# Down-projection of a hybrid decoder layer by Strassen's seven products over 1024 tokens

## Chip, cores and metric

One core of a Trainium2 chip runs the whole layer in one launch. The metric is device time in microseconds (us), the median of three runs. TensorE (PE in the profile) does the matrix products, its weight loads stand apart as PEld; VectorE is DVE, ScalarE ACT, GpSimd POOL, and SyncE (SP) issues all DMAs.

## The reference, cut to what matters

2048 tokens of width 1024; all tensors are 32-bit floats. After a mixing part (projection, short convolution, dilated attention, output projection) come the feed-forward and a gated embedding:

```python
h = rmsnorm(x, g_ffn[i])
gate = causal_dwconv3(h @ w_gate[i], ffn_conv_w[i], ffn_conv_b[i])       # 1024 -> 2816
x = x + (jax.nn.silu(gate) * (h @ w_up[i])) @ w_down[i]                  # 2816 -> 1024
ple_gate = jax.nn.sigmoid(rmsnorm(x, g_ple[i]) @ w_ple_gate[i])
x = x + ple_gate * (p[i] @ w_ple_proj[i])
```

## The kernel before

**Products.** Every operand of a product is split in two: `hi`, its rounded copy made by ScalarE (L89), and `lo`, the rest, made by a subtraction (L90) on VectorE or GpSimd. One product of 128x128 by 128x512 then takes three matmuls (`mm3`, L92): hi*hi, hi*lo, lo*hi.

**Stages.** `rest` (L649) runs the stages of the list in L651 to L653. The tokens lie in four chunks of 512 (c = 0 to 3); a half h is two chunks. `gate_up(h)` makes gates and ups of a half by Strassen-Winograd: `left` (L690) makes seven operands of a block of weights (four of them through sums on VectorE, L702), `right` (L715) makes the seven operands of h from four blocks, and `products` (L735) does the seven products of 12 matmuls each. One turn of f (11 turns) is one call of `products` for the gates and one for the ups: 14 products, 168 matmuls. On the way VectorE filters the gates (`taps`, L243: a short copy L247, two steps L255 and L256), adds products to PSUM results (L746, L940, L951) and multiplies up by gate (L949, L952). The result goes to DRAM (`gd`, L953).

**Down.** `down(c)` (L958) takes one chunk. For each half of the 1024 output columns it goes over 22 blocks f of the contraction: the block of `gd` is loaded and split (hi ScalarE, lo VectorE, tiles `g`), a block of `w_down` comes from `stream` (L610; loaded by SP, hi ScalarE, lo GpSimd, tiles `w`), and `tokens_major` (L795) does 4 x 3 = 12 matmuls into four PSUM banks. So four chunks take 4 x 2 x 22 x 12 = 2112 matmuls. At the end of a half VectorE adds the residual from PSUM (L972), SP stores it (L973) and ScalarE sums the squares (L771).

**Background.** `prepare(1)` makes the right operands for the second half (load, `normalize` L781, transposes on TensorE L792, `right`), `prepare_ple` those of `w_ple_gate`. They are generators; `step()` (L808) runs each up to its next yield, four times per half in `down`. `prepare_ple` has four yields, so all of it is issued in the first half of `down(2)`; its seven lo subtractions per block of k are all on GpSimd.

**Order.** The program order is turned into a fixed order for each engine when the kernel is built, by a planner with costs of its own; at run time each engine and the DMA queue take their instructions strictly in this order. Buffers limit how far anyone is ahead: `stream` keeps 3 operands ready, pools hold 5 `w`, 4 `g`, 10 `t`, 4 `s` and 4 `u` tiles, PSUM has 6 banks for products and 2 for transposes.

Of the kernel before, what the change touches and what calls it, by code (L numbers as in the profile page):

```python
# [39 lines left out]
class Layer:  # L40


    def __init__(self, tc, a, out, ctx):
# [14 lines left out]
        self.gd = [d.tile([NF, P, QT], F32, name=f"gd{c}") for c in range(NQ)]  # L58
# [531 lines left out]
    def weight_units(self, stages):  # L590
# [4 lines left out]
        for name, *arg in stages:  # L595
# [9 lines left out]
            elif name == "down":  # L605
                for half in range(2):
                    for u in range(NF // 2):
                        yield pair(a["w_down"], half)[u]

    def stream(self, raws, operand, left, ahead, stages):  # L610
# [3 lines left out]
        def load(src):  # L614
            if src.shape[1] == 2:
                raw = [raws.tile([P, 2, 512], F32, name="raw", tag="raw")]
# [7 lines left out]
        def made():  # L624
            units = self.weight_units(stages)
            following = load(next(units))
            while following:
                raw, src = following, next(units, None)
                following = None if src is None else load(src)
                if len(raw) == 1:  # L630
                    for i in range(2):
# [17 lines left out]
    def rest(self):  # L649
        nc, tc, a = self.nc, self.tc, self.a  # L650
        stages = [("project", (0, 1), (0,)), ("project", (0, 1), (1,)), ("prepare", 0), ("project", (2, 3), (0, 1)),  # L651
                  ("gate_up", 0), ("prepare", 1), ("down", 0), ("down", 1),
                  ("gate_up", 1), ("prepare_ple",), ("down", 2), ("down", 3), ("ple",)]  # L653
        with ExitStack() as st:
# [11 lines left out]
            pst = pool("rq", bufs=2, space=PSUM)  # L666
            psum = pool("rp", bufs=6, space=PSUM)
            new_quad = lambda i: quads[i].tile([P, 4, 2, QT], F32R, name="t", tag="t")
            bank = lambda: psum.tile([P, 512], F32, name="ps", tag="ps")
# [45 lines left out]
            def right(quad, at, b11, b12, b21, b22, temps, lo_engine):  # L715

                def put(i, x, engine):
                    hi, lo = at(quad[i])
# [8 lines left out]
                put(2, b22, lo_engine)  # L727
                minus(t2, b22, t1)
                put(6, t3, nc.gpsimd)
                put(1, b21, lo_engine)  # L730
                minus(t4, b21, t2)
                put(5, t2, nc.gpsimd)
                put(3, t4, nc.gpsimd)

# [33 lines left out]
            def add_squares(i, c, j, half, x):  # L768

                n = 4 * c + j  # L770
                nc.scalar.activation(row("u"), x, AF.Square, accum_out=sums[i][:, half, n:n + 1])  # L771
# [16 lines left out]
            def transposed(x, g):  # L788

                tp = pst.tile([P, 4, P], F32, name="tp", tag="tp")  # L790
# [4 lines left out]
            def tokens_major(pss, t, w, first, last):  # L795

                for j in range(4):
                    s = slice(j * P, j * P + P)
                    self.mm3(pss[j], t[:, 0, s], t[:, 1, s], w[:, 0], w[:, 1], first, last)
# [310 lines left out]
```

## Time and profile before

| | us |
|---|---|
| median of three runs (lowest, highest) | 2833.24 (2826.6, 2835.92) |
| profiled execution, its time | 2837.99 |
| its span, first to last instruction | 2836.1 |
| `gate_up(0)`: its products begin | 1229.69 |
| `down(0)` and `down(1)` begin, end | 1654.56, 1906.59 |
| `down(2)` and `down(3)` begin, end | 2333.26, 2603.80 |

| engine | busy, us | share |
|---|---|---|
| TensorE | 2687.8 | 95% |
| VectorE | 1941.1 | 68% |
| ScalarE | 1300.1 | 46% |
| GpSimd | 1289.7 | 45% |

Busy time counts an instruction from its start to its end, with whatever it waits for inside. In a row of the timeline the first number is the start, the second the length of a run of like instructions, xN how many they are, and the brackets the engine's idle time before them with what ended it. Groups by line give busy time, the mean ns of one, and the idle time before.

### The profile page before, as it was taken

Reading aid. Unit: us, or ns where it says so; the run is one execution under the profiler, and the core shown is the slowest. Engines: PE = TensorE matmul, PEld = TensorE weight load, DVE = VectorE, ACT = ScalarE, POOL = GpSimd, SP = SyncE. Lnnn points to the kernel's source line nnn. Section 1 sums busy time; section 2 is a strip of 40 time slices with the busy share of each in tenths; the row PEclk is TensorE's granted clock in tenths of the full one; section 3 lists DMA queues with packets and bytes.
Section 4 is the critical chain, followed back from the end, with each engine's and each line's share of the span. In section 5 each row is a group of like instructions: output and inputs, shape, how many; then the busy total and the mean of one; then the engine's idle time right before and its main releaser. Section 6 shows DMA issues by size and latency. Waiting matters only on the chain. (4 is left out here: it accounts for less than half of the span.)

```text
span 2836.1 us, 38470 instructions
## 1 busy us (share of the span) xinstructions
PE 2687.8 (95%) x12584; PEld 2226.0 (78%) x12584; DVE 1941.1 (68%) x3603; ACT 1300.1 (46%) x2727; POOL 1289.7 (45%) x916
## 2 busy tenths in 40 slices
PE   7999989999899869899999999999999998999998
PEld 5777778888788658778888888888888876888777
DVE  8776656767676545987777776657777777555644
ACT  3332257776777234543333345543333344444332
POOL 4111311624343723455445566544445559445554
PEclk9999999999899989999999999999999998999999
DMA  6444566675755779632222267652222236674342
GB/s 185 149 135 126 170 156 151 180 176 148 200 158 148 213 205 322 200 104 83 78 82 89 82 228 244 216 193 76 77 82 89 80 130 213 232 239 139 121 124 83
DMA packets 360071, 432.87 MB, mean 153 GB/s; under 512 B 49216, under 2 KB 212672, under 8 KB 359872
## 3 DMA queue, kind: packets, MB, share of 16 engines
q1 hardware_dynamic: 359872, 430.43, 49.9%
q8 instruction: 99, 1.62, 0.2%
q14 instruction: 100, 0.82, 0.1%
HBM read 335.34 MB, written 94.96 MB: 152 GB/s over the span
## 5 line engine op out<-in xcount | busy, mean ns | idle before, releaser
L93 PE MATMUL ps<-t,w 128*128 128x512 f32 x4368 | 1020.9, 394 | 5.7 <-ACT w L89 5.1
L93 PEld LDWEIGHTS ps<-t,w 128*128 128x128 f32 x4368 | 818.8, 188 | 200.2 <-DVE u L746 7.5
L90 POOL TENSOR_TENSOR w<-raw,w 128x512 fp32r<-128x512 f32 x340 | 473.1, 1395 | 475.4 <-ACT w L89 390.0
L93 PE MATMUL ps<-w,g 128*128 128x512 f32 x2688 | 637.6, 398 | 49.9 <-ACT g L817 23.2
L93 PEld LDWEIGHTS ps<-w,g 128*128 128x128 f32 x2688 | 511.1, 192 | 165.9 <-ACT g L817 25.4
L90 POOL TENSOR_TENSOR w<-s,w 128x512 fp32r<-128x512 f32 x208 | 301.3, 1449 | 255.4 <-ACT w L89 255.4
L90 DVE TENSOR_TENSOR g<-t,g 128x512 fp32r<-128x512 f32 x176 | 231.8, 1324 | 158.4 <-ACT g L89 156.6
L89 ACT CAST w<-raw 128x512 fp32r<-128x512 f32 x340 | 209.1, 616 | 284.0 <-PE ps L93 187.1
L288 POOL TENSOR_TENSOR clo<-craw,chi 128x512 fp32r<-128x512 f32 x96 | 124.8, 1306 | 393.0 <-ACT chi L287 109.5
L93 PE MATMUL zps<-hq,chi 128*128 128x512 f32 x768 | 256.5, 411 | 9.0 <-DVE ext L321 5.1
L89 ACT CAST w<-s 128x512 fp32r<-128x512 f32 x208 | 128.0, 617 | 253.5 <-PE ps L93 222.1
L438 ACT ACTIVATE pt<-so,md 128x256 f32<-128x256 f32 (+1 forms) x384 | 175.0, 457 | 84.0 <-DVE md L435 82.1
L435 DVE CUSTOM_DVE_ANT_0 so<-s,neg 128x256 f32<-128x256 f32 (+1 forms) x384 | 130.0, 361 | 61.3 <-PE s L432 49.9
L93 PEld LDWEIGHTS zps<-hq,chi 128*128 128x128 f32 x768 | 141.5, 195 | 34.7 <-DVE ext L321 6.4
L93 PE MATMUL zps<-hq,clo 128*128 128x512 f32 x384 | 154.0, 401 | 0.0
L431 PE MATMUL s<-kk,qs 128*128 128x256 f32 (+1 forms) x384 | 133.7, 355 | 19.3 <-DMA kk<-kd 17.8
L432 PE MATMUL s<-kk,qs 128*128 128x256 f32 (+1 forms) x384 | 137.7, 363 | 13.6 <-DMA v<-vd 10.3
L471 DVE TENSOR_TENSOR nb<-po,nb 64x512 f32<-64x512 f32 x96 | 92.2, 960 | 64.1 <-ACT nb L470 63.1
L172 POOL TENSOR_TENSOR raw<-hT 128x1024 f32<-128x1024 f32 x16 | 39.0, 2438 | 202.2 <-DVE rs_h L76 181.4
L932 ACT ACTIVATE t<-t 128x512 f32<-128x512 f32 x88 | 55.4, 629 | 163.9 <-DVE t L256 135.6
L431 PEld LDWEIGHTS s<-kk,qs 128*128 128x128 f32 x384 | 106.0, 277 | 26.8 <-issue 15.3
L453 DVE TENSOR_TENSOR plo<-ptp,phi 128x512 fp32r<-128x512 f32 (+1 forms) x160 | 103.6, 653 | 31.2 <-ACT phi L452 30.3
(188 smaller groups left out, 4494.4 us busy)
## 6 DMA issues: line engine op xcount, KB each, us to landing
raw<-in_w_down_dram SPq DMA_DIRECT2D x88, 512.0 KB, 3.7
t<-gd SPq DMA_DIRECT2D x176, 256.0 KB, 3.6
craw<-in_w_in_dram SPq DMA_DIRECT2D x96, 256.0 KB, 4.0
raw<-in_w_gate_dram SPq DMA_DIRECT2D x44, 512.0 KB, 3.7
raw<-in_w_up_dram SPq DMA_DIRECT2D x44, 512.0 KB, 3.5
gd<-t SPq DMA_DIRECT2D x88, 256.0 KB, 2.0
xd<-t SPq DMA_DIRECT2D x80, 256.0 KB, 4.3
t<-xd SPq DMA_DIRECT2D x76, 256.0 KB, 3.7
```

What stands on the lines that cost most here:

```text
L89: self.nc.scalar.copy(hi, src)
L90: lo_engine.tensor_tensor(lo, src, hi.bitcast(F32), ALU.subtract)
L93: mm = lambda *a, **k: self.nc.tensor.matmul(*a, **k, **kw)
L172: nc.gpsimd.tensor_tensor(t, hT[:, :, 0].bitcast(F32), hT[:, :, 1].bitcast(F32), ALU.add)
L288: nc.gpsimd.tensor_tensor(lo, raw, hi.bitcast(F32), ALU.subtract)
L431: mm(s[:, lo:], qb[l], cols[0], start=True, stop=False)
L432: mm(s[:, lo:], qb[l], cols[1], start=False, stop=True)
L435: nc.vector.tensor_tensor_reduce(out=so[:, lo:], in0=s[:, lo:], in1=neg[:, br, lo:], scale=-slope, scalar=3.0e38, op0=ALU.add, op1=ALU.min ...
L438: nc.scalar.activation(pt[:, l, lo:], so[:, lo:], AF.Exp, bias=md[:, 0, col:col + 1], scale=-1.0, accum_out=md[:, 1, col:col + 1])
L453: nc.vector.tensor_tensor(lo[:, i:i + n], tp[:, :n], hi[:, i:i + n].bitcast(F32), ALU.subtract)
L471: nc.vector.tensor_tensor(dst, like(po[other], br), dst, ALU.add)
L932: nc.scalar.activation(t, t, AF.Silu)
```

## The change

`down(h)` now takes 1024 tokens, so the product is (1024 tokens x 2816) by (2816 x 1024) in 2 x 2 blocks: two chunks of tokens, two interleaved halves of the 22 contraction blocks, two halves of the columns. It does seven products of 11 blocks each, 7 x 11 x 12 = 924 matmuls for a half.

- In `gate_up` GpSimd makes four sums and differences of the results of a turn (`combined`), and seven tensors of 128x512 per turn are stored in `gd` instead of four.
- `for_later` runs as background of `gate_up(0)`, two steps per turn: in 8 yields it normalizes and transposes the tokens of the second half and stores them (`bd`); in 11 yields it loads two blocks of `w_down`, makes four differences of 128x512 on GpSimd and stores them (`td`).
- `prepare(1)` loads `bd` instead of `xd`; it has no transposes left. `right` yields after each of its seven operands, and `down` makes four steps per product, 28 in all, which are the 28 yields of `prepare(1)` and of `prepare_ple`.
- PSUM is divided anew for `down`: two sets of four banks, used in turn. The results of products are kept in `e` tiles (`kept`); three times the four residual rows get a kept sum added on GpSimd before the product (`finished`).

```diff
-                  ("gate_up", 0), ("prepare", 1), ("down", 0), ("down", 1),
-                  ("gate_up", 1), ("prepare_ple",), ("down", 2), ("down", 3), ("ple",)]
+                  ("gate_up", 0), ("prepare", 1), ("down", 0), ("gate_up", 1), ("prepare_ple",), ("down", 1), ("ple",)]
...
-                for half in range(2):
-                    for u in range(NF // 2):
-                        yield pair(a["w_down"], half)[u]
+                b = a["w_down"].rearrange("(f i p) (s n) -> i s p f n", i=2, p=P, n=512)
+                t = [t.rearrange("f p s n -> s p f n") for t in self.td]
+                for m in (b[0, 0], t[1][1], b[1, 0], t[0][1], t[0][0], t[1][0], b[1, 1]):
+                    for f in range(0, NF // 2, 2):
+                        yield m[:, f:min(f + 2, NF // 2)]
...
+            def for_later():
+                r = roots(0, 8, 8)
+                wide = lambda: operand("g").bitcast(F32)
+                for j in range(4):
+                    for i in range(2):
+                        x = wide().rearrange("p s n -> p (s n)")
+                        nc.sync.dma_start(x, self.xd[1][2 + i][j])
+                        normalize(x, r[:, 4 * i + j:4 * i + j + 1], self.g_ffn)
+                        for g in range(2):
+                            nc.scalar.copy(x[:, 512 * g:512 * g + 512].rearrange("p (k n) -> p k n", n=P), transposed(x, g))
+                        nc.sync.dma_start(self.bd[i][j], x)
+                        yield
+                minus = lambda t, x, y: nc.gpsimd.tensor_tensor(t, x, y, ALU.subtract)
+                for f in range(NF // 2):
+                    b1, b2 = wide(), wide()
...
+                    minus(b1[:, 0], b1[:, 1], b1[:, 0])
+                    minus(b1[:, 1], b2[:, 1], b1[:, 1])
+                    minus(b2[:, 1], b2[:, 1], b1[:, 0])
+                    minus(b2[:, 0], b2[:, 0], b2[:, 1])
+                    for t, b in zip(self.td, (b1, b2)):
+                        nc.sync.dma_start(t[f], b)
+                    yield
...
                     products(ws, self.quad, gate)
+                    step()
                     products(ws, self.quad, up)
+                    step()
+                    a11, a12, a21, a22 = ts[0, 0], ts[1, 0], ts[0, 1], ts[1, 1]
+                    s1, s2, s4 = (row("t") for _ in range(3))
+                    combined(4, s1, a21, a22, ALU.add)
+                    combined(1, s2, s1, a11, ALU.subtract)
+                    combined(3, a21, a11, a21, ALU.subtract)
+                    combined(6, s4, a12, s2, ALU.subtract)
...
+                def product(pss, m, first):
+                    for f in range(NF // 2):
                         g, t = row("t"), operand("g")
-                        nc.sync.dma_start(g, self.gd[c][f])
+                        nc.sync.dma_start(g, self.gd[h][m, f])
                         self.split(t[:, 0], t[:, 1], g, nc.vector)
-                        tokens_major(pss, t, next(ws), f == 0, f == NF - 1)
-                        if f % 11 in (2, 7):
+                        tokens_major(pss, t, next(ws), first and f == 0, f == NF // 2 - 1, skip_group_check=True)
+                        if f % 3 == 1:
                             step()
+                def finished(pss, m, first, i, half, addend):
+                    c, cols = 2 * h + i, slice(512 * half, 512 * half + 512)
+                    xs = [row("s") for _ in range(4)]
+                    for j, x in enumerate(xs):
                         nc.sync.dma_start(x, self.xd[1][c][j][:, cols])
+                        if addend:
+                            nc.gpsimd.tensor_tensor(x, x, addend[j], ALU.add)
+                    product(pss, m, first)
+                    for j, x in enumerate(xs):
                         nc.vector.tensor_tensor(x, pss[j], x, ALU.add)
                         nc.sync.dma_start(self.xd[2][c][j][:, cols], x)
-                        add_squares(1, c, j, half, x)
+                        add_squares(1, c, j, half, x, row("u") if m == 4 else pss[j])
+                four = lambda n: [bank(n) for _ in range(4)]
+                x, y = four("a"), four("b")
+                product(x, 0, True)
+                for u, ps in zip(u1, x):
+                    nc.scalar.copy(u, ps)
+                product(y, 1, True)
+                for t, u, ps in zip(u2, u1, y):
+                    nc.vector.tensor_tensor(t, ps, u, ALU.add)
+                finished(x, 2, False, 0, 0, None)
+                product(y, 3, False)
+                for u, ps in zip(u1, y):
+                    nc.vector.tensor_tensor(u, ps, u, ALU.add)
+                z = four("a")
+                finished(z, 4, True, 1, 1, u1)
+                finished(four("b"), 5, True, 1, 0, u1)
+                finished(z, 6, False, 0, 1, u2)
...
```

## Rows read from the trace of the kernel before

**Rows 1.** The page, busy time, share of the span and instructions.
```profile
PE 2687.8 (95%) x12584; PEld 2226.0 (78%) x12584; DVE 1941.1 (68%) x3603; ACT 1300.1 (46%) x2727; POOL 1289.7 (45%) x916
```

**Rows 2.** Stretches: length, busy PE, PEld, DVE, ACT, POOL, granted clock, DMA share, GB/s.
```profile
1300.00:1600.00 300.00, 300.00 (x1295) 242.49 (x1294) 226.66 (x320) 112.55 (x193) 151.89 (x109) 1.00 0.26 83
...
2333.00:2406.00 73.00, 59.09 (x215) 45.90 (x216) 59.00 (x43) 34.76 (x63) 68.50 (x44) 0.86 0.66 225
2406.00:2603.00 197.00, 197.00 (x872) 163.20 (x871) 112.07 (x101) 89.47 (x167) 99.87 (x73) 1.00 0.64 216
```

**Rows 3.** Timeline of TensorE in both pairs of down stages.
```profile
1745.21 1.03 PE L792 MATMUL tp<-ident,e 128*128 128x128 f32 x8
...
1783.86 122.90 PE L93 MATMUL ps<-w,g 128*128 128x512 f32 x541
...
2319.67 10.73 PE L93 MATMUL ps<-t,w 128*128 128x512 f32 x45
2333.26 6.41 PE L93 MATMUL ps<-w,g 128*128 128x512 f32 x20 [2.85 <-ACT g L89]
...
2371.04 4.61 PE L93 MATMUL ps<-w,g 128*128 128x512 f32 x12 [2.03 <-POOL w L90]
...
2399.66 5.49 PE L93 MATMUL ps<-w,g 128*128 128x512 f32 x12 [5.63 <-POOL w L90]
...
2406.04 197.92 PE L93 MATMUL ps<-w,g 128*128 128x512 f32 x872
```

**Rows 4.** What TensorE waited for from 2300 to 2610: total, times, longest.
```profile
PE ps L93 <- POOL w L90: 11.9, 6, 5.6
```

**Rows 5.** Timeline of POOL, then DVE, from 2370 to 2384.
```profile
2377.69 3.42 POOL L90 TENSOR_TENSOR t<-u,t 128x512 fp32r<-128x512 f32 x2
2381.07 3.43 POOL L90 TENSOR_TENSOR w<-raw,w 128x512 fp32r<-128x512 f32 x2
...
2379.89 1.77 DVE L722 TENSOR_TENSOR u<-e 128x512 f32<-128x512 f32 x1
2381.59 1.77 DVE L722 TENSOR_TENSOR u<-e,u 128x512 f32<-128x512 f32 x1
```

**Rows 6.** Line L539, a 128x512 product on GpSimd: ns shortest/median/longest.
```profile
L539 POOL TENSOR_TENSOR yt<-nb,wb x14: 1263/1290/1742, 538.8 to 987.1; 128x512 f32<-128x512 f32 x14
```

**Rows 7.** Groups by line in gate_up(0), 1300 to 1600: busy us, mean ns.
```profile
L90 POOL TENSOR_TENSOR w<-s,w 128x512 fp32r<-128x512 f32 x62 | 90.9, 1466 | 69.0 <-ACT w L89 69.0
L90 POOL TENSOR_TENSOR w<-raw,w 128x512 fp32r<-128x512 f32 x47 | 62.3, 1325 | 80.1 <-ACT w L89 45.0 <-DVE u L746 35.1
...
L256 DVE SCALAR_TENSOR_TENSOR t<-e,fcw,t 128x512 f32<-128x512 f32 x30 | 37.0, 1233 | 0.6
L255 DVE SCALAR_TENSOR_TENSOR t<-e,fcw,t 128x512 f32<-128x512 f32 x30 | 34.1, 1137 | 9.3 <-ACT t L254 9.3
L952 DVE TENSOR_TENSOR t<-u,t 128x512 f32<-128x512 f32 x24 | 31.6, 1315 | 0.5
...
L247 DVE COPY e<-e 128x62 f32<-128x62 f32 x30 | 25.8, 860 | 0.2
...
L702 DVE TENSOR_TENSOR s<-raw 128x512 f32<-128x512 f32 x31 | 21.1, 682 | 0.0
L746 DVE TENSOR_TENSOR u<-ps,u 128x512 f32<-128x512 f32 x31 | 21.0, 679 | 0.0
...
L951 DVE TENSOR_TENSOR u<-ps,u 128x512 f32<-128x512 f32 x24 | 16.5, 687 | 10.2 <-PE ps L93 9.9
L940 DVE TENSOR_TENSOR e<-ps,u 128x512 f32<-128x512 f32 x22 | 15.2, 689 | 18.1 <-PE ps L93 17.9
L702 DVE TENSOR_TENSOR s<-raw,s 128x512 f32<-128x512 f32 x16 | 15.0, 940 | 9.5 <-POOL w L90 9.5
L702 DVE TENSOR_TENSOR s<-s,raw 128x512 f32<-128x512 f32 x16 | 11.1, 693 | 24.4 <-POOL w L90 24.4
```

**Rows 8.** Stores of the down stages (L973): from issue to landing.
```profile
DMA to landing us min/median/max: 2.0/3.7/6.5
```

More of the change, by code (lines that the diff above doesn't have):

```diff
@@ L630, in made @@
                 if len(raw) == 1:
-                    for i in range(2):
+                    for i in range(raw[0].shape[1]):
                         t = operand()
@@ L665, in rest, with divide @@
             tiles = pool("re", bufs=4, side="right")
-            pst = pool("rq", bufs=2, space=PSUM)
-            psum = pool("rp", bufs=6, space=PSUM)
+            banks = {}
+            def divide(**counts):
+                if banks:
+                    banks.pop("stack").close()
+                banks["stack"] = inner = ExitStack()
+                for n, k in counts.items():
+                    banks[n] = inner.enter_context(tc.tile_pool(reuse_waits="tile", name="r" + n, bufs=k, space=PSUM))
+            divide(p=6, q=2)
+            st.callback(lambda: banks["stack"].close())
             new_quad = lambda i: quads[i].tile([P, 4, 2, QT], F32R, name="t", tag="t")
-            bank = lambda: psum.tile([P, 512], F32, name="ps", tag="ps")
+            bank = lambda n="p": banks[n].tile([P, 512], F32, name="ps", tag="ps")
             row = lambda tag: (rows if tag == "t" else small).tile([P, 512], F32, name=tag, tag=tag)
@@ L766, in rest, with add_squares @@
             sums = [cp.tile([P, 2, 4 * NQ], F32, name=f"sums{i}") for i in range(2)]
[L768 removed]
+            def add_squares(i, c, j, half, x, junk):
                 n = 4 * c + j
[L771 removed]
+                nc.scalar.activation(junk, x, AF.Square, accum_out=sums[i][:, half, n:n + 1])
             def roots(i, first, n):
@@ L788, in transposed @@
             def transposed(x, g):
-                tp = pst.tile([P, 4, P], F32, name="tp", tag="tp")
+                tp = banks["q"].tile([P, 4, P], F32, name="tp", tag="tp")
                 for k in range(4):
@@ L955, in gate_up @@
                     products(ws, self.quad, gate)
+                    step()
                     products(ws, self.quad, up)
-            def down(c):
-                for half in range(2):
-                    cols = slice(512 * half, 512 * half + 512)
-                    pss = [bank() for _ in range(4)]
-                    for f in range(NF):
+                    step()
+                    a11, a12, a21, a22 = ts[0, 0], ts[1, 0], ts[0, 1], ts[1, 1]
+                    s1, s2, s4 = (row("t") for _ in range(3))
@@ new lines, in gate_up, with down @@
+                    combined(4, s1, a21, a22, ALU.add)
+                    combined(1, s2, s1, a11, ALU.subtract)
+                    combined(3, a21, a11, a21, ALU.subtract)
+                    combined(6, s4, a12, s2, ALU.subtract)
+            def down(h):
+                divide(b=4, a=4)
+                kept = [tiles.tile([P, D], F32, name="e", tag="e") for _ in range(4)]
+                u1, u2 = [[t[:, i:i + 512] for t in kept[n:n + 2] for i in (0, 512)] for n in (0, 2)]
+                def product(pss, m, first):
+                    for f in range(NF // 2):
@@ L976, in prepare_ple @@
+                divide(p=6, q=2)
             def prepare_ple():
@@ L1015, in operands @@
                         blocks.append([t[:, 0], t[:, 1]])
-                    tp = pst.tile([P, 4, P], F32, name="tp", tag="tp")
+                    tp = banks["q"].tile([P, 4, P], F32, name="tp", tag="tp")
                     for k in range(4):
@@ L1060, in rest @@
             for name, *arg in stages:
+                if name not in ("project", "down"):
+                    for _ in background[0]:
+                        pass
                 if name.startswith("prepare"):
@@ L1063, in rest @@
                     continue
-                if name in ("gate_up", "ple"):
-                    for _ in background[0]:
-                        pass
                 run[name](*arg)
```

78 lines of the change are left out of this document (51 added, 27 removed).

## The prediction, made before the changed kernel ran

> **What bounds the kernel now.** I read the page's busy times first: TensorE 2687.8 of 2836.1 us, all others below 70% [rows 1]. Then the stretches, because a mean over stages can hide a second bound. In `gate_up(0)` TensorE is busy for all of 300 us, with GpSimd at half and VectorE at three quarters; the back of the last two `down` stages is the same, 197.00 of 197.00 [rows 2]. The timeline gives the price of a matmul: 122.90 us for 541 and 197.92 for 872, so 0.227 us in `down` [rows 3]; in `gate_up` 300/1295 = 0.232, and a turn of 168 is 38.9 us [rows 2].
>
> One stretch of the stages touched is different. From 2330.4 (the end of the 45 matmuls before `down(2)`) to 2406.04 the timeline has gaps [rows 3], 11.9 us of them ended by GpSimd's `w` [rows 4], and the mean granted clock is 0.86 [rows 2]: after several waits of TensorE a part of the stretch runs at 1.2 instead of 2.4 GHz, and 12 matmuls take 4.61 us there instead of 2.73 [rows 3]. In it lie 184 matmuls of `down`, 24 of `gate_up` and 8 transposes: 184 x 0.227 + 24 x 0.232 + 1.0 = 48.4 us of work in 75.6 us. So 27.2 us are lost there. What is issued there is all of `prepare_ple`, 28 lo subtractions on GpSimd beside those that `down` needs.
>
> Why GpSimd is late: in this stretch it and VectorE take turns. VectorE's subtractions of two SBUF tiles take 1.77 us instead of the 0.68 us that the like take at L702, and two GpSimd subtractions take 3.42 us, that is 1.69 each [rows 5, 7], where the shortest GpSimd operation of this size takes 1.26 [rows 6]. A pair costs 1.69: I count 1.26 for GpSimd's and 0.43 for VectorE's. VectorE's additions that read PSUM (L746, L951, L940) stay at 0.68 to 0.69 beside all this [rows 7] and don't count. The stretch of 73 us holds 44 GpSimd and 43 VectorE operations [rows 2]: 44 x 1.26 + 43 x 0.43 = 74 us. The shared time was full; this is the second bound.
>
> **The change part by part.**
>
> *Matmuls removed.* 2112 become 2 x 924 = 1848, each of the same form. 264 x 0.227 = 59.9 us, all on the path, since TensorE is the bound there.
>
> *Background of the last `down`.* The four yields of `prepare_ple` in the first 22 blocks become 28 yields over 77 blocks. Per block GpSimd has one `w` and VectorE one `g`: 1.69 of 2.73 us, 62%. `prepare_ple` adds 28 x 1.26 + 16 x 0.43 = 42 us over a stage of 924 x 0.227 = 210, 20%; the 12 additions in `finished` 15 us, 7%. Together 89%: the 27.2 us go. In `down(0)` the load is less (16 GpSimd and 28 VectorE operations of `prepare(1)`, 15%). I leave 4 us for both, because the additions come four at a time ahead of a product's own `w`; bounds 0 and, if the crowding stays, 27.2.
>
> *Banks.* Each product has four banks and the next has the other four; results are read in some 2.8 us (4 x 0.69) of the 30 us (132 x 0.227) of the next product. No cost.
>
> *Transposes.* 64 move from `down` to `gate_up(0)`. Eight take 1.03 us [rows 3], so 64 are 8.2 us, which are paid before and after alike. They now follow their `normalize` in the same yield; TensorE waits if VectorE is behind the planned order. Eight such places; 0 to 2 us each; I take 3 in all.
>
> *`gate_up(1)`.* Per turn there are 14 GpSimd operations (109 in 300/38.9 = 7.7 turns) and 19 VectorE ones that count (30 + 30 + 24 + 31 + 16 + 16 over 7.7, the short copies L247 left out) [rows 7]. Shared time before: 14 x 1.26 + 19 x 0.43 = 25.8 of 38.9 us, 66%. Four `combined` add 5.0: 79%. Three more stores per turn go to a queue at 26% DMA share [rows 2]. The burst of four takes 4 x 1.69 = 6.8 us, and the operands ready ahead cover four products, 4 x 12 x 0.232 = 11 us. I take 3 us, near the lower bound of 0, since the shared time has a fifth to spare; the upper one, if each of the 18 GpSimd operations holds up one of VectorE's, is 42 (worked out at rival D).
>
> *`gate_up(0)`.* The same, and the background. Turns 0 to 3 get two `normalize` each, on VectorE, counted as two 512s each, 1.7 us: 32.6 of 41.0 us (with 16 transposes). No loss. From turn 4 on, for 5.5 turns, two yields of `for_later` add eight differences: 26 GpSimd operations, 25.8 + 5.0 + 10.1 = 41.0 us of shared time in a turn of 38.9. TensorE is late by at least 5.5 x 2.1 = 12 us, minus what buffers hold. Above: VectorE's queue is in order, and the additions that free PSUM stand behind the operations that wait. If all 19 pay the 1.77 of the alternating stretch [rows 5], four L247 their mean of 0.86 and 10 PSUM additions (31 + 24 + 22 over 7.7) 0.68 each [rows 7], VectorE needs 43.9 us per turn, 5.0 over TensorE's 38.9, 27 us over 5.5 turns. I take 18, nearer to the lower end: the stretch at 2330 had an excess of 74 - 48 = 26 us of shared time and lost 27.2, little more than the excess.
>
> The Trainium skill, in "SBUF — State Buffer", section "SBUF: two separate sides", says that GpSimd and a VectorE instruction with two SBUF inputs shut each other out of a common port pair for the whole instruction. That it is either one or the other the trace shows; that it is the whole is not borne out: 1.26 + 0.68 would make 1.94 a pair, and the rows have 1.69. By the whole length the sum below would come to 2799 us (rival B).
>
> *Ends of `down`.* The `s` tiles of the last `finished` are held until their stores land, 3.7 us [rows 8], and `left` needs the first of them for the second operand of the next stage. The first bank is done 9 matmuls (2.0 us) before the end; + 0.7 addition + 3.7 landing + two sums (1.4) and a rounding on ScalarE, taken like a sum (0.7), + lo 1.3 = 5.8 us after the end, and the first operand's product covers 2.8. So 3 us at each of two ends, 6 us; bounds 0 (another order) and, with the clock falling, 12. At the start of `down` such gaps were there before too (2.85 [rows 3]).
>
> *Sum.* -59.9 - 27.2 + 4 + 3 + 3 + 18 + 6 = -53.1. The profiled execution took 2837.99 us (span 2836.1), so 2784.9; the median of the runs is 4.75 below it: 2780 us.
>
> **The rivals.**
>
> A, the ports cost nothing: buffers and idle slots take up `gate_up(0)`'s excess, and the ends are planned around. Then -87.1 + 5 from 2837.99, less the 4.75: 2751. For: no wait of TensorE in 300 us with VectorE at 76% [rows 2]. Against: 41.0 in 38.9.
>
> B, GpSimd and VectorE shut each other out for the whole length of both instructions: a crowded turn then needs 26 x 1.26 + 19 x 0.68 = 45.7 us, 6.8 over, 37 us over 5.5 turns instead of 18: 2799. For: 1.77 us of VectorE beside GpSimd; against: 1.69 a pair [rows 5].
>
> C, `gate_up(0)` pays the upper bound and the crowding of `prepare_ple` moves on instead of going, because 89% is a mean and the additions bunch: +9 and +20, 2809. For: the tight stretch filled 100%. Against: spread over three and a half times as many blocks.
>
> D, slower: VectorE becomes the bound of both `gate_up` stages. With no operation held up, a turn of VectorE is (19 + 10) x 0.68 + 4 x 0.86 = 23.1 us [rows 7]; every one that is held up adds 1.77 - 0.68 = 1.09. So TensorE is reached at 15 of 19 per turn, and the saving is used up at 18 in every turn of both stages (74 us over 22 turns are 3.4 per turn above 38.9). With 18 held up a turn is 42.7 us, 3.8 x 11 = 42 for a stage; with all, 5.0 x 22 = 110 us in place of the 21: 2869. For: operations of GpSimd go from 14 to 18 and 26 per turn. Against: VectorE's 29.4 us per turn now (226.66/7.7 [rows 2]) mean 6 held up by 14; at that rate 26 make 11, and 18 make 8.
>
> E, the change doesn't do what it says: a matmul costs more in the new order, and the 60 us come back, 2840, no change. For: `gate_up`'s cost 0.232 against 0.227. Against: form, tiles and source of operands stay.
>
> **Chances.** The forecast 0.50 (2765 to 2792), A 0.13, B 0.14, C 0.11, D 0.07, E 0.05. A measurement of this kernel tells about 0.3%, 8.5 us, from no change. Faster takes the forecast, A, B and most of C, which has some 15 us to the 2824.7 where no change begins: 0.86. Same is E and the rest of C, less some of E that ends slower: 0.06. Slower is D and that part of E: 0.08. The range goes from A's 2750 to 2826, past C; above it lie D and E, below it a part of A.
>
> **What would show it.** 1848 matmuls of `down` at 0.227; no gaps and clock 1.00 at the start of the second `down`; in turns 4 to 9 of `gate_up(0)` waits of TensorE for GpSimd's `w` or VectorE's PSUM additions, with GpSimd near 100% and VectorE's two-tile operations at 1.7 us; `gate_up(1)` at 428 us plus a little; gaps of about 3 us at the ends of `down`. Wrong would be: `gate_up(0)` longer than 428 + 8 + 45 us, `gate_up(1)` longer by over 15, or gaps inside `down`.

## The result, and the profile after

The changed kernel took 2873.1 us (2869.56 to 2883.12, four runs) where the one before took 2834.58 beside it: the ratio of the means of the runs is 1.0146, its 95% interval 1.0112 to 1.0179. It is slower by 1.5%. The forecast of 2780, its range and its sign were wrong.

The profiled execution is the longest of the four (2883.12 us) and has a span of 2881.3 us, 45.2 more than before. Here are its stages, each from the first matmul of its products to the first of the next stage, beside the terms of the prediction; the last two columns are of experiments told below (e10 computes no differences of `w_down`, e15 is the whole computation in another order):

| change of the span, us | predicted | after | e10 | e15 |
|---|---|---|---|---|
| all that runs before `gate_up(0)` | 0 | +21.3 | +2.2 | +6.2 |
| `gate_up(0)`, and the wait until `down` | +29.2 | +63.9 | +19.0 | +24.0 |
| first `down` | -33.1 | -31.1 | -42.6 | -42.6 |
| `gate_up(1)`, and the wait until `down` | +3 | +23.7 | +12.6 | +12.0 |
| second `down`, until `ple` | -52.2 | -37.4 | -49.1 | -47.6 |
| `ple` | 0 | +4.9 | +0.8 | +2.1 |
| sum | -53.1 | +45.2 | -57.1 | -45.9 |

(Predicted: 8.2 us of transposes go from the first `down` to `gate_up(0)`; 59.9, 4 and 6 are halved over the two `down`. The rows are rounded one by one.)

One thing in the rows is only a shift. In the kernel before, the last 24 matmuls of each `gate_up` ran behind the first ones of `down`, and count there; in the changed kernel they run ahead of it. So 5.6 us of what each `gate_up` gains in the table, and of what each `down` loses, are these. From the kernel before:

```profile
1659.76 5.60 PE L93 MATMUL ps<-t,w 128*128 128x512 f32 x24
...
2339.50 5.60 PE L93 MATMUL ps<-t,w 128*128 128x512 f32 x24
```

The page's busy times, beside [rows 1]: TensorE has 264 matmuls less and is busy for 27.5 us less, not 60; GpSimd gained 227 us.

```profile
PE 2660.3 (92%) x12320; PEld 2194.4 (76%) x12320; DVE 2017.7 (70%) x3597; ACT 1291.1 (45%) x2699; POOL 1516.8 (53%) x1050
```

TensorE's timeline shows where it stood: in the last blocks of the projection (8.33 and 4.50), for VectorE's PSUM additions in `gate_up(0)` (4.01 and 6.67 are the longest), and 15.55 and 12.36 us ahead of the two `down`, where the kernel before had 1.17 and 2.85 (the second stands in [rows 3]).

```profile
1191.17 2.88 PE L812 MATMUL tp<-ident,e 128*128 128x128 f32 x12 [8.33 <-DVE rsy L853]
...
1207.94 43.17 PE L95 MATMUL ps<-w,g 128*128 128x512 f32 x182 [4.50 <-DVE g L838]
...
1417.61 5.49 PE L95 MATMUL ps<-t,w 128*128 128x512 f32 x12 [4.01 <-DVE u L766]
...
1465.09 36.02 PE L95 MATMUL ps<-t,w 128*128 128x512 f32 x144 [6.67 <-DVE u L766]
...
1739.69 35.63 PE L95 MATMUL ps<-w,g 128*128 128x512 f32 x146 [15.55 <-ACT g L91]
...
1960.62 2.88 PE L95 MATMUL ps<-t,w 128*128 128x512 f32 x12
1963.92 0.73 PE L95 MATMUL ps<-t,w 128*128 128x512 f32 x2 [0.41 <-ACT w L91]
1965.83 8.16 PE L95 MATMUL ps<-t,w 128*128 128x512 f32 x34 [1.18 <-POOL w L92]
1976.02 416.01 PE L95 MATMUL ps<-t,w 128*128 128x512 f32 x1776 [2.03 <-DVE u L766]
...
2411.01 24.98 PE L95 MATMUL ps<-w,g 128*128 128x512 f32 x98 [12.36 <-ACT g L91]
...
2460.42 131.53 PE L95 MATMUL ps<-w,g 128*128 128x512 f32 x579 [0.65 <-POOL w L92]
...
2641.51 3.67 PE L812 MATMUL tp<-ident,e 128*128 128x128 f32 x16 [2.80 <-ACT ps L791]
```

The 579 matmuls show the prediction's price: 131.53 / 579 = 0.227 us per matmul of `down`.

The stretches (columns as in [rows 2]) show one in `gate_up(0)` in which GpSimd is busy for 171.82 of 190 us at 117 operations, and the head of the second `down`, where it is busy for 58.04 of 60, followed by one where it is idle for half the time. Before, `gate_up(0)` had 109 operations in 300 us, and TensorE no wait [rows 2].

```profile
1360.00:1550.00 190.00, 171.23 (x709) 135.97 (x708) 156.09 (x168) 64.57 (x109) 171.82 (x117) 0.94 0.61 210
...
2411.00:2471.00 60.00, 56.56 (x228) 45.27 (x229) 47.59 (x32) 32.28 (x59) 58.04 (x36) 0.93 0.71 238
2471.00:2531.00 60.00, 60.00 (x266) 49.74 (x265) 34.06 (x31) 27.57 (x52) 28.48 (x22) 1.00 0.70 239
```

What GpSimd does in the first of them, and one group of VectorE's (groups by line, as [rows 7]):

```profile
L965 POOL TENSOR_TENSOR g<-g 128x512 f32<-128x512 f32 x44 | 65.9, 1502 | 9.1 <-DMA g<-in_w_down_dram 8.8
L92 POOL TENSOR_TENSOR w<-s,w 128x512 fp32r<-128x512 f32 x33 | 49.8, 1512 | 5.9 <-ACT w L91 5.4 <-PE ps L95 0.2
L1018 POOL TENSOR_TENSOR t<-t 128x512 f32<-128x512 f32 x16 | 24.1, 1517 | 0.0
...
L715 DVE TENSOR_TENSOR s<-raw 128x512 f32<-128x512 f32 x16 | 23.3, 1453 | 10.2 <-POOL w L92 10.2
```

All 44 differences (L965) lie here. Of the 709 matmuls 24 are transposes, so the stretch is 685/168 = 4.08 turns: 10.8 differences per turn and not the 8 of the program. VectorE's sums (L715) take 1453 ns where before they took 682 [rows 7].

### The profile page after: what moved, and what is told of

Its sections match the earlier page's. It is cut to its first block, busy times and chain, and to the rows that moved or that the text cites. A ratio compares the mean times of both kernels' runs of the same rounds, so it can differ in the third digit from the quotient of the medians.

```text
span 2881.3 us, 38272 instructions
## 1 busy us (share of the span) xinstructions
PE 2660.3 (92%) x12320; PEld 2194.4 (76%) x12320; DVE 2017.7 (70%) x3597; ACT 1291.1 (45%) x2699; POOL 1516.8 (53%) x1050
## 5 line engine op out<-in xcount | busy, mean ns | idle before, releaser
L95 PE MATMUL ps<-t,w 128*128 128x512 f32 x4368 | 1040.9, 398 | 37.1 <-DVE u L766 19.1
L95 PE MATMUL ps<-w,g 128*128 128x512 f32 x2424 | 581.5, 401 | 77.3 <-ACT g L91 27.9
L95 PEld LDWEIGHTS ps<-w,g 128*128 128x128 f32 x2424 | 465.2, 194 | 187.5 <-ACT g L91 29.0
L91 ACT CAST w<-raw 128x512 fp32r<-128x512 f32 x318 | 196.0, 617 | 242.9 <-PE ps L95 157.6
L92 DVE TENSOR_TENSOR g<-t,g 128x512 fp32r<-128x512 f32 x154 | 207.8, 1360 | 126.4 <-ACT g L91 123.0
L433 PE MATMUL s<-kk,qs 128*128 128x256 f32 (+1 forms) x384 | 134.4, 356 | 21.3 <-DMA kk<-kd 20.2
L1018 POOL TENSOR_TENSOR t<-t 128x512 f32<-128x512 f32 x88 | 126.5, 1449 | 5.9 <-DVE t L1010 3.2
L455 DVE TENSOR_TENSOR plo<-ptp,phi 128x512 fp32r<-128x512 f32 (+1 forms) x160 | 103.7, 654 | 32.0 <-ACT phi L454 31.1
```

Of the source, the lines that this page charges most:

```text
L91: self.nc.scalar.copy(hi, src)
L92: lo_engine.tensor_tensor(lo, src, hi.bitcast(F32), ALU.subtract)
L95: mm = lambda *a, **k: self.nc.tensor.matmul(*a, **k, **kw)
L433: mm(s[:, lo:], qb[l], cols[0], start=True, stop=False)
L455: nc.vector.tensor_tensor(lo[:, i:i + n], tp[:, :n], hi[:, i:i + n].bitcast(F32), ALU.subtract)
L1018: nc.gpsimd.tensor_tensor(t, x, y, op)
```

## The experiments

Each is told against the changed kernel. They ran beside the kernel before, and are compared by the ratio of the means to it, with its 95% interval in brackets; 0.01 is 28 us. What a single edit gains is the difference of two such ratios, and is known to about 0.004, 11 us. How long a stage takes is given from the start of its first matmul to the start of its last.

**e1.** The projection's sums of squares.

```diff
-                                        add_squares(0, c, j, half, x, pss[j])
+                                        add_squares(0, c, j, half, x, row("u"))
```

> One edit of the changed kernel undone: in project the squares' junk goes to a row tile again, not into the product's PSUM bank. Theory (banks held until ScalarE has squared hold up project's next products and change the planned order there): the first gate_up matmul, at 1251 us in the changed kernel and 1230 before, comes at about 1236, and the whole takes about 2858 instead of 2873. Rival (the 21 us are the run's own scatter, or come from the other edits): the first gate_up matmul stays at 1245 or later, the whole within 5 us of 2873.

2860.92 us, 1.0078 (1.0057 to 1.0100). `gate_up(0)` begins at 1232.07 instead of 1250.95, and the wait of 8.33 is 1.23:

```profile
1187.31 1.45 PE L812 MATMUL tp<-ident,e 128*128 128x128 f32 x8 [1.23 <-DVE rs_y L87]
...
1232.07 14.06 PE L95 MATMUL ps<-t,w 128*128 128x512 f32 x60
```

ScalarE writes squares that nobody reads; the change had given them the product's own PSUM bank as a place. That bank then comes free only after ScalarE, and the planned order around the last blocks is another. TensorE itself stands for such a square only once, 1.5 us; how the rest follows from the bank through the planned order isn't shown, only that it goes with this one word. It cost 19 us in a stage that the prediction took as untouched.

**e2.** The first loads of a `down`.

```diff
-                        g, t = row("t"), operand("g")
+                        g, t = row("t" if m else "s"), operand("g")
```

> Only the 11 gd blocks of down's first product are loaded into s tiles instead of t tiles. Theory (the t tiles of the first blocks are handed out after those of the last turn's three sums, so the loads stand behind the last results of gate_up in SyncE's queue): the gaps of 15.6 and 12.4 us ahead of the two down stages shrink to 3 us or less, and the whole takes about 2849. Rival (the first operands of prepare(1), or the late sums themselves, hold up the first splits in the queues of ScalarE and VectorE): the first gap stays over 10 us, since these still stand ahead.

2860.89 us, 1.0080 (1.0052 to 1.0108). The gaps of 15.55 and 12.36 are 1.99 and none:

```profile
1725.51 16.00 PE L95 MATMUL ps<-w,g 128*128 128x512 f32 x62 [1.99 <-ACT t L91]
...
2387.94 12.40 PE L95 MATMUL ps<-w,g 128*128 128x512 f32 x54
```

That is 26 us less of gaps, and 19 us by the ratio: `gate_up(0)` and the first `down` took 3 to 4 us longer each (476.2 and 224.3 instead of 472.8 and 220.7).

Why, SP's timeline shows: in the changed kernel the loads (L1041, of `t`) stand behind the stores of the last turn's results and sums (L1015), since `t` tiles go from one user to the next in program order:

```profile
1725.78 0.32 SPq L1015 DMA_DIRECT2D gd<-t  x1
...
1731.27 1.99 SPq L1015 DMA_DIRECT2D gd<-t  x2
1733.31 0.92 SPq L1041 DMA_DIRECT2D t<-gd  x2
```

In e2 the first load, of an `s` tile, is issued at 1699.22, ahead of such a store:

```profile
1699.22 0.32 SPq L1041 DMA_DIRECT2D s<-gd  x1
1700.48 0.32 SPq L1015 DMA_DIRECT2D gd<-t  x1
1703.61 7.32 SPq L1041 DMA_DIRECT2D s<-gd  x5
```

**e3.** No differences of `w_down` in `gate_up(0)`.

```diff
-                minus = lambda t, x, y: nc.gpsimd.tensor_tensor(t, x, y, ALU.subtract)
+                minus = lambda t, x, y: None
```

> The 44 differences of w_down blocks on GpSimd are left out, so the output is not the reference's; their loads and stores stay. Theory (GpSimd and VectorE shut each other out, and 26 GpSimd operations per turn overfill that time): gate_up(0), 473 us from its first matmul to its last in the changed kernel, falls to 445, with hardly a wait of TensorE for VectorE's u (L766) in turns 4 to 9; the whole about 2845. Rival (23 MB of added loads and stores in SyncE's queue delay the weights): gate_up(0) stays over 465, since they are all there.

2845.98 us, 1.0024 (1.0010 to 1.0037). `gate_up(0)`, from its first to its last matmul, takes 441.7 us instead of 472.8; its work is 1848 x 0.2317 + 8.2 = 436.4. The loads and stores of this background are all still there, so their traffic is not what it costs. (GpSimd's waits at the differences for loads that haven't landed, 8.8 us, are gone with the differences, though; e7 is without them too.) What TensorE still waits for there (total, times, longest):

```profile
PE ps L95 <- POOL w L92: 2.4, 2, 1.5
PE ps L95 <- DVE u L766: 1.4, 3, 0.9
```

**e4.** The differences on VectorE:

```diff
-                minus = lambda t, x, y: nc.gpsimd.tensor_tensor(t, x, y, ALU.subtract)
+                minus = lambda t, x, y: nc.vector.tensor_tensor(t, x, y, ALU.subtract)
```

> The 44 differences are made on VectorE instead of GpSimd. Theory (shared time is the limit; 1.26 us of GpSimd become 0.43 of VectorE, 41.0 becomes 34.3 of 38.9 us in a crowded turn): gate_up(0) falls from 473 to about 450, the whole to about 2850. Rival (VectorE's queue in order is the limit, and gets 8 x 0.68 = 5.4 us more per turn): gate_up(0) stays at 473 or grows, with more waits for VectorE's u (L766).

2867.86 us, 1.0106 (1.0081 to 1.0131); `gate_up(0)` 466.5 us, between the two expectations. GpSimd is down to 112.61 of 190 us, and still TensorE waits 12.8 us in the stage for `u`, VectorE's PSUM additions (13.8 in the changed kernel). So GpSimd's fullness alone isn't the cause. But VectorE now stands 11.9 us itself at the differences, for their loads, so that this run doesn't tell the one delay of its queue from the other.

```profile
1358.00:1548.00 190.00, 172.79 (x724) 137.07 (x723) 165.97 (x222) 64.81 (x110) 112.61 (x75) 0.96 0.62 212
```

**e5.** Background of `down` held to its step: what is issued after a step may not be planned ahead of the matmul at which the step stands.

```diff
-                    self.split(hi, lo, x, engine)
+                    paced(nc.scalar.copy(hi, x))
+                    engine.tensor_tensor(lo, x, hi.bitcast(F32), ALU.subtract)
...
-                minus = lambda t, x, y: nc.vector.tensor_tensor(t, x, y, ALU.subtract)
+                minus = lambda t, x, y: paced(nc.vector.tensor_tensor(t, x, y, ALU.subtract))
```

(`paced` adds an order dependency on the last matmul before the step.)

> Only the background of the down stages is tied to its step: each rounding and difference that right issues in a step may be planned no sooner than the matmul at that step. Theory (the planner draws the 28 yields together: in the changed kernel 21 of prepare_ple's 28 GpSimd subtractions run in the first 60 us of the second down stage, as they did before the change): the second down stage, 227 us from its first to its last matmul against 210 of work, falls to about 215, the first from 221 to about 215, the whole to about 2855. Rival (the additions of finished and the shared time as such are the cause): both stay within 4 us of what they are.

2850.43 us, 1.0054 (1.0035 to 1.0073); the two `down` take 210.9 and 215.8 us instead of 220.7 and 227.3, of 924 x 0.227 = 209.7 each. In the second 878 of the 924 matmuls run without a stop, and the head has 28 GpSimd operations in 60 us instead of 36:

```profile
2385.32 201.95 PE L95 MATMUL ps<-w,g 128*128 128x512 f32 x878 [9.05 <-ACT g L91]
```
```profile
2386.00:2446.00 60.00, 60.00 (x256) 49.39 (x255) 31.99 (x27) 31.10 (x57) 39.35 (x28) 0.96 0.73 247
```

In the changed kernel 21 of `prepare_ple`'s 28 subtractions on GpSimd lie between 2398 and 2457, and the other seven between 2579 and 2602. The yields were spread over 77 blocks, the instructions weren't: the planner draws what is ready forward.

**e6.** Blocks of `w_down` for the differences loaded one yield ahead:

```diff
-                for f in range(NF // 2):
-                    b1, b2 = wide(), wide()
...
+                following = blocks(0)
+                for f in range(NF // 2):
+                    (b1, b2), following = following, blocks(f + 1) if f + 1 < NF // 2 else None
```

> The two w_down blocks of for_later are loaded one yield ahead of their differences; the differences stay where they are. Theory that a part of the loss in gate_up(0) is GpSimd standing at a difference whose load has not landed (9 us in three waits of the changed kernel's trace), with the weights' lo behind it: gate_up(0) falls from 473 to about 462. Rival (the shared time is overfull in any case, the waits only take the place of other waits): it stays within 4 us of 473.

2879.33 us, 1.0155 (1.0138 to 1.0172); `gate_up(0)` 474.8. No gain. But the edit didn't bring what it was to test: the order planned for GpSimd stayed, and it waits for the loads for 11.0 us where it was 8.8 (group L965 above). So e6 doesn't settle what these waits cost.

```profile
POOL g L965 <- DMA g<-in_w_down_dram: 11.0, 4, 5.7
```

**e7.** Four differences in every one of the 11 turns instead of eight in 5.5, tied to the matmul at their step by `paced` (the normalizations are moved into the turn's other step):

```diff
-                minus = lambda t, x, y: nc.gpsimd.tensor_tensor(t, x, y, ALU.subtract)
+                minus = lambda t, x, y: paced(nc.gpsimd.tensor_tensor(t, x, y, ALU.subtract))
...
                     products(ws, self.quad, gate)
+                    mark[0] = newest[0]
                     step()
```

> The differences of for_later are spread: four per turn over all 11 turns, each tied to the matmul at its step, the normalized tokens in the turns' other step. Theory (26 GpSimd operations in a turn overfill the shared time, 22 do not: 25.8 + 5.0 + 5.0 = 35.9 of 38.9 us): gate_up(0) falls from 473 to about 445, as near as the kernel without differences, and the whole to about 2848. Rival (VectorE's own queue in order is the limit, with 22 GpSimd operations a turn it still pays in each turn): 460 or more.

2887.84 us, 1.0191 (1.0176 to 1.0207); `gate_up(0)` 484.2. It was to be shorter. No difference waits for its load any more, and `gate_up(0)` loses without such waits too. TensorE now waits once in nearly every turn, for VectorE; three of these stops, of 3.15, 3.80 and 3.80 us, come after the last normalization, so they don't hang on the normalizations either:

```profile
PE ps L95 <- DVE u L776: 31.7, 10, 3.8
```

One such place, in the timelines of GpSimd, VectorE and TensorE:

```profile
1455.22 1.75 POOL L966 TENSOR_TENSOR g<-g 128x512 f32<-128x512 f32 x1
1457.06 1.57 POOL L92 TENSOR_TENSOR w<-s,w 128x512 fp32r<-128x512 f32 x1
```
```profile
1454.03 1.79 DVE L258 SCALAR_TENSOR_TENSOR t<-e,fcw,t 128x512 f32<-128x512 f32 x1
1455.73 1.78 DVE L715 TENSOR_TENSOR s<-raw 128x512 f32<-128x512 f32 x1
1457.45 1.24 DVE L249 COPY e<-e 128x62 f32<-128x62 f32 x1
...
1459.34 0.68 DVE L776 TENSOR_TENSOR u<-ps,u 128x512 f32<-128x512 f32 x1
```
```profile
1460.07 2.50 PE L95 MATMUL ps<-t,w 128*128 128x512 f32 x5 [3.14 <-DVE u L776]
```

The PSUM addition (L776) takes 0.68 us even here, but stands in VectorE's order behind three operations that wait for GpSimd: L715 takes 1.78 us where it takes 0.68 alone [rows 7]. The four differences of the turn lie within 11 us here (they begin at 1446.4, 1447.8, 1450.7 and 1455.2), with `lo` subtractions of the weights between them, so that GpSimd stands idle among them only once, for 1.46 us; TensorE stops for 3.14.

**e8 and e11.** e11 is e1, e2 and e5 together; e8 is these and e7's order.

> All that helped in its own stage at once: squares' junk in rows, first loads of down in s tiles, down's background and the differences tied to their steps. If the losses are separate and add up, -18 -22 -15 -25 us on 2873: about 2793, and 1.5% faster than the kernel before. If one bound lies behind all of them and the time moves to the next wait, it stays above 2830, no faster than before.

> The same three edits alone, differences on GpSimd as in the changed kernel. If the losses are separate: 2873 - 18 - 19 - 22 = 2814, 0.7% faster than before, gate_up(0) at 473. If the three share a cause, 2830 or more.

e11: 2809.64 us, 0.9910 (0.9891 to 0.9928), 4 us under what was expected. e8: 2823.93 us, 0.9956 (0.9940 to 0.9972); its `gate_up(0)` of 489.7 against e11's 475.0 is the difference. So e8 met neither of its expectations: the three losses are separate, but e7's order, which was to give 25 us, costs 13.

**e9 and e10.** e11 with VectorE's differences (e4) and without differences (e3).

> Squares' junk in rows, first loads of down in s tiles, down's background tied to its steps, and the differences on VectorE, where the planner puts them. If the gains of the single runs add up (-18, -19, -22, -10 us), about 2804 and 1% faster than the kernel before, with gate_up(0) at 466. If VectorE's differences collide with the changed order ahead of gate_up, 2820 or more.

> The same three edits, and the 44 differences left out, so the output is not the reference's. This closes the account: if gate_up(0) is all that keeps the change from the 2780 us that were forecast, it falls to about 441 us and the whole to about 2778. If something else is still lost (added stores, the sums on GpSimd, the last stage), it stays above 2795.

e9: 2803.35 us, 0.9881 (0.9857 to 0.9904). e10: 2779.94 us, 0.9806 (0.9784 to 0.9828), its `gate_up(0)` 443.7. Both came within 2 us of what was expected. The causes add up: from the change's 1.0146, e1 takes 0.0068, e2 0.0066, e3 0.0122, e5 0.0092, together 0.0348; e10, which has all four, is 0.0340 lower.

**e12.** The additions that free PSUM, split into a copy by ScalarE and an addition from SBUF.

```diff
-                    nc.vector.tensor_tensor(t, ps, x, ALU.add)
+                    nc.scalar.copy(t, ps)
+                    nc.vector.tensor_tensor(t, t, x, ALU.add)
```

> In products the two sums with u1 (L766) are made in two steps: ScalarE copies the bank to SBUF, VectorE adds there. So TensorE waits for a ScalarE copy instead of VectorE's queue before it goes on in that bank; VectorE gets two more operations with two SBUF inputs per call. Theory (the loss in gate_up(0) is lateness in VectorE's queue: the addition that frees the bank stands behind operations that wait for GpSimd): waits of TensorE in gate_up(0) mostly go, and it falls from 473 to 450 or less. Rival (the shared time is overfull, the place of the wait is secondary): 468 or more, with waits for GpSimd's w or for later sums in their place.

2897.58 us, 1.0218 (1.0197 to 1.0239); `gate_up(0)` 491.3 and, without any background, `gate_up(1)` 455.8 instead of 437.6. The waits of TensorE for the bank went to others; in `gate_up(1)`:

```profile
PE ps L95 <- POOL w L92: 14.2, 6, 2.4
```

Ahead of the first of its stops of 2.36 us GpSimd stands 2.56 us for VectorE's product (`t`) and then makes three sums in 4.75 us, before the `lo` that TensorE waits for. Whether that comes of the four more operations per turn on two SBUF tiles or of the order that was planned anew, this run doesn't tell. My theory that only the order of VectorE's queue mattered was wrong as put.

**e13 and e15.** e11, and the differences one at a time: a step after each of the 14 products of a turn, each difference tied to another matmul; GpSimd in e13, VectorE in e15. Two things come with it: the blocks are loaded three products ahead of their first difference, and each normalization is split over three steps.

```diff
+                    mark[0] = (r.ins if hasattr(r, "ins") else r).name
+                    step()
+                    mark[0] = None
...
-                minus = lambda t, x, y: nc.gpsimd.tensor_tensor(t, x, y, ALU.subtract)
+                minus = lambda t, x, y: paced(nc.gpsimd.tensor_tensor(t, x, y, ALU.subtract))
```

> With the three edits (squares in rows, first loads in s tiles, paced down): for_later in steps after each of the 14 products of a turn, so the four GpSimd differences of a turn stand apart, each tied to another matmul. Theory (what costs is the bunch: GpSimd operations back to back hold up VectorE's queue longer than a bank can wait, 22 in a turn would fit): gate_up(0), 475 us with the three edits alone, falls to 455 or less, the whole to about 2790. Rival (the shared time of GpSimd and VectorE is too full whatever the order, as adding VectorE operations in products showed): 470 or more.

> As the run with differences one at a time, but on VectorE, which has the shared ports for a third of the time per difference. If order and shared time both matter, this is the shortest of the kernels that compute all: gate_up(0) about 450 us against 467 with all of VectorE's differences where the planner puts them, the whole about 2785 against 2803. If VectorE's queue is the limit it stays at 465 or more.

e13: 2789.61 us, 0.9825 (0.9809 to 0.9842), `gate_up(0)` 452.1. e15: 2788.24 us, 0.9825 (0.9811 to 0.9840), 448.6. Either is 1.75% faster than the kernel before, and between them there is no difference that can be told. In neither does a difference wait for its load any more. In e13 GpSimd does 161 operations in 300 us, and TensorE's waits in `gate_up(0)` are few:

```profile
1300.00:1600.00 300.00, 293.08 (x1270) 233.20 (x1270) 264.43 (x317) 116.78 (x197) 229.33 (x161) 0.99 0.50 170
```
```profile
PE ps L95 <- DVE u L777: 5.7, 4, 2.5
PE ps L95 <- POOL w L92: 4.4, 7, 0.6
```

e8 against e13 tells best what the order is worth: four differences per turn on GpSimd in both, none of which waits for its load, and `gate_up(0)` 489.7 us with the four together, 452.1 with them apart. In e15 against e9 (467.2) the loads are a second reason: VectorE stood 8.3 us for them in e9.

**e14.** e11 without the four sums per turn (the stores stay).

```diff
-                        nc.gpsimd.tensor_tensor(t, x, y, op)
-                        keep(m, t)
+                        keep(m, ts[0, 0])
```

> With the three edits: the 88 sums of gate_up on GpSimd are left out (a gate's result is stored in their place), so the output is not the reference's; the 44 differences stay. It prices the sums: if four GpSimd operations per turn cost time even where the shared time is below 80%, gate_up(1) falls from 439 us to about 429 and gate_up(0) from 475 to about 450. If sums cost nothing where there is room, gate_up(1) stays at 437 or more and only gate_up(0) falls.

2809.69 us, 0.9901 (0.9878 to 0.9923) against e11's 0.9910: no gain. `gate_up(1)` takes 438.7 us with sums left out and 439.0 with them. The sums aren't what it lost. `gate_up(0)`, which was to fall to about 450, takes 471.8 where e11 took 475.0. The planner draws the differences closer still, all 44 into 155 us (187 in e11), and TensorE stands as before, with GpSimd busy for 79% only (it stands 15.0 us for the differences' loads):

```profile
1340.00:1530.00 190.00, 170.65 (x720) 134.87 (x719) 153.36 (x177) 65.68 (x110) 150.70 (x103) 0.96 0.63 213
```

## Why the prediction was wrong

**Right: the matmuls.** 264 less at 0.227 us. Once the losses below are taken away (e10, e15), the first `down` takes 209 us for its 924 matmuls and the second 213 to 214, where 924 x 0.227 is 209.7.

**Failed: "Together 89%: the 27.2 us go".** The step spread 28 yields over 77 blocks and took their instructions to be spread as well. The planner drew 21 of 28 into 60 us, where GpSimd was busy for 58.04. That is the second half of rival C, the crowding that moves on: the two `down` took 220.7 and 227.3 us of 209.7 of work, and holding the instructions to their step (e5) gave 26 us back, 21 of them in these two stages.

**Failed: the start of `down`, costed at nothing because "such gaps were there before too".** They were of 1.17 and 2.85 and became 15.55 and 12.36. I had counted the three more stores per turn by the share of the queue, not by which `t` tiles they hold: the first loads of `down` need such a tile. Worth 19 us (e2).

**Failed: "No cost" for the banks.** The step looked at the results of products in `down` and not at ScalarE's squares, which the change had put into their banks. In the projection, which the prediction leaves out, that is worth 19 us (e1); at the end of the second `down` TensorE stands 2.80 us for such squares.

**Place right, size and reckoning off: `gate_up(0)`, "I take 18".** From its first to its last matmul it took 472.8 us; less the work of 436.4 that is 36, against 18 + 3. The shared time was worked out for 8 differences per turn over 5.5 turns; they came as 10.8 over 4.1. In the full stretch 117 operations of GpSimd and 76 of VectorE on two SBUF tiles (L257, L258, L715, L1010) make 117 x 1.26 + 76 x 0.43 = 180 of 190 us, 95%. e3 shows that the differences are the cause (35 us by the ratio, 31 in the stage).

What failed is the step from shared time to lost time. By the same price the 300 us from 1300 to 1600 are filled in e7 to 82% (151 operations of GpSimd and 128 of VectorE) and in e13 to 88% (161 and 142); over the work of 436.4 e7 loses 48 us and e13 16. So it isn't the excess over a turn that is lost. How close the operations follow one another decides, since VectorE's PSUM additions stand in line behind what waits for GpSimd; the prediction had this queue only in its upper bound of 27.

The Trainium skill, in "SBUF — State Buffer", section "SBUF: two separate sides", has GpSimd and a VectorE instruction with two SBUF inputs shut each other out for the whole instruction. By it the full stretch would hold 117 x 1.26 + 76 x 0.68 = 199 us in 190 (VectorE's 0.68 is the duration of [rows 7]), so the trace doesn't bear out the whole length; e13's 161 and 142 of them would nearly fill 300 (299), and TensorE waited there for little. Rival B's 37 us would still have come nearer to 36 than 18 did, but not for its own reason, since it too reckons by an excess over the turn.

**Ends of `down`, "3 us at each".** Behind the first, TensorE goes on without a stop and then stands 0.41 and 1.18 us at the second operand, where the wait was put. But the four stores landed in 2.1 us and not in 3.7, and VectorE's sum (L715) began at 1961.66, right behind the additions (until 1961.57). Behind the second it stands the 2.80 us for squares, and the first product's matmul comes 6.6 us after the last of `down`, where it was 1.0 before. 1.6 and 5.6 us are near the 6 in sum, by chance.

**Too low: `gate_up(1)`, "I take 3".** 437.6 us from its first to its last matmul, against 428.2 + 3. Of the 9.4 us over its work 4.5 are stops: those of 0.41 and 1.18, one of 2.03 behind them and one of 0.87 ahead of the last 24 matmuls. The rest lies in the 1776 matmuls without a stop, which took 416.01 us where 1776 x 0.2317 is 411.5. Without the sums it isn't less (e14); what else lengthens this run, no run here tells.

**The rivals.** D's 2869 is nearest to what was measured, and by luck: it puts 110 us into the two `gate_up` stages, which lost 36 and 9, and nothing into the projection and the starts of `down`.

That e10 comes to 2779.94, the very forecast, is chance too: it computes no differences, for which 18 had been allowed, and loses 14 us elsewhere beyond what the sum has there (8 in `gate_up(1)`, 4 in `gate_up(0)`, 2 ahead of it). The whole computation in the best order found, e15, takes 2788.24, inside the range of 2750 to 2826. Between the kernel that ran and this one lie 19 + 19 + 26 us for places and order in three stages, and 24 for a bunch (e11 to e13): 88 of the 91 that the ratios are apart.

Open: behind the second `down` of e10 TensorE still stands 5.29 us for ScalarE's squares in PSUM ahead of `ple`. No run takes these away.

```profile
2543.51 3.40 PE L820 MATMUL tp<-ident,e 128*128 128x128 f32 x16 [5.29 <-ACT ps L799]
```

## What to carry to other kernels

When a planner or scheduler sets the order, a mean load over a stage (89% here) doesn't tell what it costs: ask what holds an added instruction back to its place, and if nothing does, price it as a bunch at the start. Follow each added store to the tile it holds and to the next load that wants that tile, and each scratch output to the buffer that it keeps from others. Work on a resource that two engines share was cheap one instruction at a time and dear close together (16 and 48 us for the same 44 differences), because a queue in order makes everybody behind the waiting one late, also those that don't need the resource.

## What was not expected of the hardware

- Which of the two engines waits goes by which began first. In e13 GpSimd's operation of 128x512 takes 1.29 us when it begins first, and VectorE's on two SBUF tiles, begun 0.08 us later, takes 1.76; the next of GpSimd begins while that one is under way and takes 1.74. GpSimd, then VectorE:

```profile
1404.12 1.73 POOL L92 TENSOR_TENSOR w<-s,w 128x512 fp32r<-128x512 f32 x1
1405.81 1.29 POOL L1044 TENSOR_TENSOR t<-t 128x512 f32<-128x512 f32 x1
1407.06 1.74 POOL L968 TENSOR_TENSOR g<-g 128x512 f32<-128x512 f32 x1
```
```profile
1403.70 1.00 DVE L1036 TENSOR_TENSOR t<-u,t 128x512 f32<-128x512 f32 x1
1405.89 1.76 DVE L715 TENSOR_TENSOR s<-raw,s 128x512 f32<-128x512 f32 x1 [1.18 <-POOL w L92]
```

- VectorE's short copies wait too, though they read one tile, and the prediction left them out of the shared time. In e7 a copy of two columns (L255) takes 0.17 us at 1452.02, and 1.26 at 1449.47, until a GpSimd operation ends (1449.40 and 1.31). In the full stretch of the changed kernel 40 such copies (L249, L253, L255) keep VectorE for 32.6 of the 190 us.

```profile
1449.40 1.31 POOL L92 TENSOR_TENSOR w<-s,w 128x512 fp32r<-128x512 f32 x1
```
```profile
1449.47 1.26 DVE L255 COPY fcarry<-e 128x2 f32<-128x2 f32 x1
...
1452.02 0.17 DVE L255 COPY fcarry<-e 128x2 f32<-128x2 f32 x1
```

- A stop of TensorE cost more than its length, and short ones cost about as much more as a long one. Behind the gap of 15.55 (mean granted clock 0.61 from 1723 to 1739.5) the 146 matmuls take 35.63 us where 146 x 0.227 = 33.1, at a mean clock of 0.94. In e2, behind stops of 1.80 and 1.99, the same 146 take 35.7, of which 0.37 is a stop, at 0.95.
- Neither engine's busy share told what TensorE loses: in the 190 us GpSimd is busy for 171.82 and VectorE for 156.09 in the changed kernel, 150.70 and 153.36 in e14, and TensorE does 171.23 and 170.65 us of work. Its waits are put down to VectorE for the most part (11.3 of 18.8 us in the changed kernel).
